# Expert weights in 1 MB loads of two rows to a partition, with every second factor column

## The chip, the cores and the metric

The kernel runs on one core of one Trainium2 chip. TensorE (PE) multiplies; VectorE (DVE), ScalarE (ACT) and GpSimd (POOL) do the elementwise work; SyncE (SP) issues most of the DMA transfers, and 16 DMA engines move the bytes between HBM and the on-chip SBUF. The metric is the device time of one execution in microseconds.

## What is computed

A two-layer transformer block in fp32 on 512 latent tokens (x) and 256 context tokens (ctx), 1024 wide. Each layer has a mixer (layer 0: dense attention and a convolution; layer 1: windowed attention and pooling) and then a mixture of experts with two of 32 experts for each token:

```python
def _moe(h, grp_w, grp_b, exp_w, exp_b, w_gate, w_up, w_down):
    ...  # a group of 8 experts by argmax, in it the two best, with weights
    def run(args):
        tok, wt, e = args
        xb = h_pad[tok]
        hid = jax.nn.silu(xb @ w_gate[e]) * (xb @ w_up[e])
        return (hid @ w_down[e]) * wt[:, None]
    ...

def reference(...):
    for i in range(DEPTH):              # 2
        ...                             # modulation from c, mixer, residual
        hx = _modulate(_rmsnorm(x, ln2_g[i]), sh2, sc2)
        ...
        x = x + g2 * out                # layer 0: 768 tokens; layer 1: 512
```

An expert has two factors of 1024 x 512 (w_gate, w_up) and one of 512 x 1024 (w_down), 6.3 MB; 32 experts are 201 MB a layer, and all of them are read.

## The kernel before

The order of the work is written out by hand on every engine, except that in two regions (layer 1's attention is one) PE, DVE and POOL are placed by a scheduler. The parts follow each other: mixer of layer 0, experts of layer 0, mixer of layer 1, experts of layer 1.

**Pages.** Large operands lie in SBUF pages of 128 x 1024 fp32 (4 KB to a partition, 512 KB). Class Pages keeps a list of free ones: 22 of pool keep for the whole program (R), and others that a part adds (T for 9 or 11 and S for 9 or 6 during the experts, by NT and NS; M and E in the mixer of layer 1). Pages.new takes the first that fits; Pages.done gives one back, and the next user of that place waits for the old one's readers. Weights, activations X, the fp32r parts hi and lo (class Split), attention outputs oT and a row g2b all live in such pages.

**Expert weights.** The host lays an expert out as 12 pages: chunks 0 and 1 (gate and up, 4 pages each, one page for 128 rows of the factor, with 256 gate and 256 up columns twice) and chunk 2 (down, 4 pages). Experts.queue lists all 384 pages of a layer in the order of use. Experts.ahead takes pages from that list as long as places are free and has SP issue one DMA for each (L1342):

```python
n, i, p = self.queue.pop(0)
t = pages.new("w", pools=self.pools)
queue.dma_start(t, a["ex"][self.l, order[n], i, p])
```

It is called while the mixer still runs (extra_slot, before_experts: FIRST and G1 say how many pages), and then each time pages were used: in layer 0 (main0) after all 8 pages of gate and up, and after the 4 of down; in layer 1 (main1, used_page) after each page.

**An expert.** Rows of its tokens come by an indirect DMA that POOL issues (gather, L1367) into Xg. In transposed, 8 PE transposes (L1476) turn them into xt, 128 features to a block; in layer 1 the modulation is applied while they are copied out of PSUM (modulate_T, L689 and L691, factors from A2s and modT). mm_gate_up (L1492) multiplies: for each of 8 blocks k of features and both halves c of the array, the stationary operand is 64 tokens of xt, the moving one 512 columns of page k. hidden applies silu and the product; hidden_T (L1506) transposes the result in blocks of 128; mm_down (L1514) does the same with the 4 pages of down. An fp32 matmul is two PE instructions; the two halves c run side by side. In layer 0 an expert has a second block of tokens if more than 64 came to it, and results go by scatters (POOL, L1394) that add to xD in HBM. In layer 1 two experts' results are added to X by one-hot products (combine, L1440).

**Layer 1's start.** The end of its mixer (OutProj) interleaves with the routing of each token tile. SP's queue there holds expert pages, g1b (a row that DVE waits for, L636), more pages, g2b, and then all others. On POOL, rs (L266) of each tile and the running sums of the routing precede the first gather.

Of the kernel before, what the change touches and what calls it, by code (L numbers as in the profile page):

```python
# [7 lines left out]
F32 = mybir.dt.float32  # L8
# [36 lines left out]
G1 = 3  # L45
FIRST = ((11, 0, 2), (7, 3, 2))

NT = (9, 11)
NS = (9, 6)
# [21 lines left out]
def hybrid_dit_kernel(ctx: ExitStack, tc: tile.TileContext, a, out):  # L71
# [27 lines left out]
    class Pages:  # L99
# [3 lines left out]
        def __init__(self):  # L103
            self.free, self.held, self.first = [], {}, None

        def add(self, pool, name, n):
            self.free += [(pool, f"{name}{i}") for i in range(n)]

        def drop(self, pool):
            self.done([t for t, p in list(self.held.values()) if p[0] is pool])  # L110
            self.free = [p for p in self.free if p[0] is not pool]

        def new(self, name, dt=F32, shape=(128, PAGE), pools=None):
            fit = [i for i, p in enumerate(self.free) if pools is None or p[0] in pools]
            i = next((i for i in fit if self.free[i][0] is self.first), fit[0])
            pool, tag = place = self.free.pop(i)
            t = pool.tile(list(shape), dt, tag=tag, name=name, bufs=1)
            self.held[id(t)] = (t, place)
            return t

        def done(self, tiles):
            for t in tiles:
                self.free.append(self.held.pop(id(t))[1])
# [112 lines left out]
    def mod_rows(l, name, src):  # L236
# [5 lines left out]
        for r in range(2):  # L242
            nc.sync.dma_start(rowD[l][name][r].rearrange("(k n) -> k n", n=128), g[r:r + 15:2, :])
# [35 lines left out]
    class Split:  # L279
# [15 lines left out]
        def low(self, t, eng=nc.vector):  # L295
            lo = pages.new("wl", F32R)
# [384 lines left out]

    def modulate_T(l, r, h, ps, dst):

        for i in range(4):
            k = h * 4 + i
            src = ps[:, i * 128:(i + 1) * 128]
            g, b = A2s[l][:, k, r:r + 1], modT[:, l, 24 + k, r:r + 1]
            if i % 2:
                nc.vector.tensor_scalar(dst[:, k, :], src, g, b, op0=OP.mult, op1=OP.add)  # L689
            else:  # L690
                nc.scalar.activation(dst[:, k, :], src, AF.Identity, bias=b, scale=g)  # L691
# [444 lines left out]
    class Router:  # L1136
# [107 lines left out]
        def slots(self, pool, work, room):  # L1244
# [3 lines left out]
            if self.l == 1:  # L1248
                self.iota = pool.tile([128, nt * 128], F32, name="iotaf")
                it = work.tile([128, nt * 128], I32, tag="ys", name="iotai", bufs=1)  # L1250
# [21 lines left out]
            def products():  # L1272
# [13 lines left out]
                pages.done([room])  # L1286
# [34 lines left out]

    class Experts:
        def __init__(self, l, nt, pools):
# [6 lines left out]
            self.queue = [(n, i, p) for n, i in self.queue + [(NE - 1, 2)] for p in range(4)]  # L1330
# [138 lines left out]
        def transposed(self, src, b, xt=None):  # L1469
# [3 lines left out]
            for h in range(2):  # L1473
                ps = sm("xtp")
                for k in range(4):
                    nc.tensor.transpose(ps[:, k * 128:(k + 1) * 128], src[:, (h * 4 + k) * 128:(h * 4 + k + 1) * 128], ident)  # L1476
                if self.l == 1:
                    modulate_T(1, 0, h, ps, xt)
# [8 lines left out]

        def mm_gate_up(self, b, xt, q, w, beside=lambda k: None):
# [22 lines left out]
        def mm_down(self, yy, b, t, w, beside=lambda f: None):  # L1511
            for f in range(4):
                for c in range(2):
                    nc.tensor.matmul(yy[c * 64:(c + 1) * 64], t[:, b, f % 2, f // 2, :],  # L1514
                                     w[f][:, c * 512:(c + 1) * 512], start=(f == 0), stop=(f == 3))
                beside(f)

        def begin(self):
# [6 lines left out]
            room = pages.new("slots", BF, (128, 2 * PAGE))  # L1525
# [30 lines left out]
        def main0(self):  # L1556
# [38 lines left out]
            pages.done(self.g2b)  # L1595
# [617 lines left out]
```

## Time and profile before

| | us |
|---|---|
| median of three runs | 1738.57 (1738.44 to 1743.09) |
| the profiled execution | 1740.23 |
| its span, first to last instruction | 1738.6 |
| PE busy | 1555.6 (89%) |
| DVE, ACT, POOL busy | 871.4, 498.0, 430.3 |
| mean granted TensorE clock | 0.965 of full speed |
| bytes moved by DMA | 518.65 MB, 488.58 MB of it on SP's queue |

Most durations here are from the one profiled execution. Its layer stages, read from when the expert products run: mixer of layer 0 until about 450 us, experts until about 955 us, mixer of layer 1 until about 1250 us, experts until the end. PE counts as busy while a matmul waits in its pipeline for data that a later one needs, so a full PE is not PE at its full pace; instructions in a stretch say more of its pace.

### The profile page before, as it was taken

The numbers are of one execution on the slowest core, as the hardware profiler recorded it, in microseconds if no ns is written. First come the engines' busy times: TensorE is split into PE (matmuls) and PEld (weight loads), VectorE is DVE, ScalarE is ACT, GpSimd is POOL, SyncE is SP. The second block draws the span as 40 slices with busy tenths as digits, with TensorE's granted clock in tenths as the row PEclk, the third lists the DMA queues.
The fourth block names the chain that finished last, engine by engine and source line by source line (L and its number), as shares of the span: only waits on it lengthen the run. The fifth ranks groups of instructions, "written<-read, shape, count | busy, mean of one in ns | idle before, by whom it ended". The sixth has DMA issues, their size and how long they took to land. (4 is left out here: it accounts for less than half of the span.)

```text
span 1738.6 us, 23632 instructions
## 1 busy us (share of the span) xinstructions
PE 1555.6 (89%) x8524; PEld 823.2 (47%) x8524; DVE 871.4 (50%) x1674; ACT 498.0 (29%) x998; POOL 430.3 (25%) x376
## 2 busy tenths in 40 slices
PE   5979689998799999999987589989699999999996
PEld 4868457887333333333322477668433343232332
DVE  3797889788333332233232565775533443343334
ACT  3422458833111111111111443482211211111111
POOL 2535555132122122112111222310112212121110
PEclk9999889999799999999999899999799999999998
DMA  9211833356899999999999524623899999999996
GB/s 369 64 65 69 314 135 147 110 197 238 333 392 398 400 385 383 397 388 389 397 394 397 218 74 181 239 89 131 319 410 409 408 409 408 408 408 408 408 410 235
DMA packets 151567, 518.65 MB, mean 298 GB/s; under 512 B 22444, under 2 KB 23180, under 8 KB 151436
## 3 DMA queue, kind: packets, MB, share of 16 engines
q1 hardware_dynamic: 136748, 488.58, 71.8%
q0 software_dynamic: 11520, 16.81, 3.7%
q10 hardware_dynamic: 3168, 11.54, 1.7%
q8 instruction: 79, 1.29, 0.3%
q14 instruction: 52, 0.43, 0.1%
HBM read 510.49 MB, written 21.02 MB: 306 GB/s over the span
## 5 line engine op out<-in xcount | busy, mean ns | idle before, releaser
L1492 PE MATMUL gu<-w,xt 128*64 128x512 f32 x2304 | 535.4, 602 | 23.4 <-DMA w<-in_ex_dram 19.1
L1492 PEld LDWEIGHTS gu<-w,xt 128*64 128x64 f32 x2304 | 151.2, 137 | 348.1 <-issue 240.8
L1514 PE MATMUL yy<-w,ht 128*64 128x512 f32 x1152 | 272.5, 608 | 15.4 <-DMA w<-in_ex_dram 6.6
L1499 DVE TENSOR_TENSOR hh<-hh,gu 128x512 f32<-128x512 f32 (+1 forms) x64 | 35.4, 553 | 356.2 <-ACT hh L1498 356.2
L1498 ACT ACTIVATE hh<-gu 128x512 f32<-128x512 f32 (+1 forms) x64 | 31.4, 490 | 612.5 <-PE gu L1492 336.9
L1514 PEld LDWEIGHTS yy<-w,ht 128*64 128x64 f32 x1152 | 78.1, 138 | 183.5 <-issue 133.3
L1394 POOL DMA_INDIRECT xD<-ys,sidx x40 | 71.1, 1777 | 317.0 <-DVE ys L1390 314.5
L1405 DVE TENSOR_TENSOR X<-X,cmb 128x512 f32<-128x512 f32 x126 | 79.6, 683 | 99.9 <-PE cmb L1440 99.8
L1424 POOL TENSOR_TENSOR lo<-ys,hi 64x512 fp32r<-64x512 f32 x58 | 72.5, 1268 | 217.0 <-ACT hi L1423 217.0
L1367 POOL DMA_INDIRECT Xg<-hD,gidx x40 | 41.9, 1048 | 263.2 <-PE xtp L1476 243.6
L751 DVE SCALAR_TENSOR_TENSOR acc<-glu,convp,acc 128x784 f32<-128x784 f32 x76 | 97.9, 1288 | 1.6
L762 POOL TENSOR_TENSOR part<-part,prod 128x784 f32<-128x784 f32 x40 | 84.7, 2118 | 43.2 <-ACT prod L761 42.3
L1390 DVE TENSOR_TENSOR ys<-yy,ys 128x512 f32<-128x512 f32 x64 | 44.3, 692 | 96.9 <-PEq L1305 52.8
L266 POOL TENSOR_TENSOR rs<-ms,mhalf 128x1 f32<-128x1 f32 (+2 forms) x40 | 41.4, 1036 | 170.8 <-DVE ms L264 170.2
L1423 ACT ACTIVATE hi<-ys 64x512 fp32r<-64x512 f32 x64 | 40.2, 629 | 139.7 <-DVE ys L1401 139.7
L524 PE MATMUL ptp<-cst,P 128*128 128x128 f32 x368 | 52.9, 283 | 18.6 <-POOL P L512 10.5
L1508 DVE COPY ht<-htp 128x512 f32<-128x512 f32 (+1 forms) x64 | 35.4, 553 | 66.6 <-PE htp L1506 66.6
L697 PE MATMUL qps<-wh,hi 128*128 128x256 f32 (+1 forms) x176 | 61.0, 347 | 8.0 <-DVE hi L1863 2.4
L532 ACT ACTIVATE pT<-ptp 128x512 f32<-128x512 f32 (+1 forms) x96 | 53.3, 589 | 44.8 <-PE ptp L524 44.1
L512 POOL TENSOR_SCALAR P<-P,rd 128x768 f32<-128x768 f32 (+3 forms) x40 | 33.2, 829 | 130.9 <-DVE rd L510 41.9
L502 ACT ACTIVATE P<-S,nm 128x768 f32<-128x768 f32 (+3 forms) x80 | 59.9, 757 | 13.1 <-DVE nm L495 8.3
L495 DVE TENSOR_REDUCE nm<-S 128x1 f32<-128x768 f32 (+3 forms) x80 | 58.6, 763 | 8.2 <-PE S L488 5.9
(310 smaller groups left out, 2551.2 us busy)
## 6 DMA issues: line engine op xcount, KB each, us to landing
w<-in_ex_dram SPq DMA_DIRECT2D x768, 512.0 KB
w<-in_mod_w_dram SPq DMA_DIRECT2D x96, 512.0 KB
w<-in_w_out_dram SPq DMA_DIRECT2D x16, 512.0 KB
w<-in_w_in_ab_dram SPq DMA_DIRECT2D x14, 512.0 KB
hD<-x ACTq DMA_DIRECT2D x8, 512.0 KB
xD<-X ACTq DMA_DIRECT2D x6, 512.0 KB
w<-in_w_in_cd_dram ACTq DMA_DIRECT2D x6, 512.0 KB
X<-xD SPq DMA_DIRECT2D x6, 512.0 KB
```

The source lines that it names most:

```text
L495: nc.vector.tensor_reduce(nm, u["S"][h][:, u["span"]], AX.X, OP.max, negate=True)
L502: nc.scalar.activation(u["P"][h][:, :n], u["S"][h][:, u["span"]], AF.Exp, bias=nm, accum_out=u["den"][:, h:h + 1])
L524: nc.tensor.transpose(ps[:, (c - c0) * 128:(c - c0 + 1) * 128], u["P"][c // nk][:, c % nk * 128:(c % nk + 1) * 128], ident)
L532: nc.scalar.activation(dst, src, AF.Copy)
L697: nc.tensor.matmul(ps[:, o:o + n], h(x, k, tk), w(p, k, 0, n), start=(k == 0 and c == 0), stop=(k == KT - 1 and c == 2))
L751: nc.vector.scalar_tensor_tensor(acc, glu[:, ct, i:i + CW], w(i), acc, OP.mult, OP.add)
L762: nc.gpsimd.tensor_tensor(self.part[ct], self.part[ct], t, OP.add)
L1394: return nc.gpsimd.indirect_dma_start(out=xD[:, :], out_offset=bass.IndirectOffsetOnAxis(ap=idx, axis=0), in_=ys[:, :], in_offset=None, bo ...
L1405: nc.vector.tensor_tensor(x, x, ps, OP.add)
L1424: eng.tensor_tensor(lo[rows, c], ys[rows, c], hi[rows, c].bitcast(F32), OP.subtract)
L1492: nc.tensor.matmul(self.gu[c * 64:(c + 1) * 64, b, :], xt[:, k, q * 64:(q + 1) * 64], w[k][:, c * 512:(c + 1) * 512], start=(k == 0), stop ...
L1514: nc.tensor.matmul(yy[c * 64:(c + 1) * 64], t[:, b, f % 2, f // 2, :], w[f][:, c * 512:(c + 1) * 512], start=(f == 0), stop=(f == 3))
```

## The change

Two pages of a chunk are now loaded by one DMA of 1 MB. A partition p takes rows 2p and 2p + 1 of a stretch of 256 rows of the factor, which lie behind each other in HBM: a run of 8 KB to a partition where two of 4 KB were. A matmul contracts 128 rows at a time, so the moving operand of block k is now the even or the odd rows of such a stretch (second_rows), and the features of block k must be every second column: the transposes read every second column of Xg and hh (every_second). In layer 1 the modulation factors then belong to other partitions; the rows A2 and B2 are written to HBM in the mixer and read back in that order into gb on POOL's queue.

SBUF places are now 8 KB to a partition with two halves. Experts.ahead takes whole places (Pages.pair); a page elsewhere takes a half, with rules on which half shares a tile with which. Counts change: G1, FIRST, NT, NS. Pages are given back by pairs in layer 1. g2b and slots no longer lie in pages. The last chunk of modulation weights in layer 1's mixer comes as three pages and a fourth after the loop.

```diff
-G1 = 3
-FIRST = ((11, 0, 2), (7, 3, 2))
-
-NT = (9, 11)
-NS = (9, 6)
+G1 = 2
+FIRST = ((5, 0), (3, 2))
+
+NT = (8, 10)
+NS = (8, 6)
...
     def add(self, pool, name, n):
-        self.free += [(pool, f"{name}{i}") for i in range(n)]
+        self.free += [(pool, f"{name}{i}", h) for i in range(n // 2) for h in range(2)]
+        if n % 2:
+            self.free.append((pool, f"{name}odd", 0))
...
+        def take(self, name, place, halves, dt):
+            if not self.used(place):
+                n = PAGE * (1 if place[1].endswith("odd") else 2)
+                self.base[place] = place[0].tile([128, n], dt, tag=place[1], name=name, bufs=1), dt, name
+            h = halves[0] * PAGE
+            t = self.base[place][0][:, h:h + PAGE * len(halves)]
...
+        def pair(self, pools):
+            t, places = self.take("w", self.whole(pools)[0], (0, 1), F32)
+            self.held[id(t)] = (t, places)
+            return t
...
+    def every_second(src, k):
+        return src.rearrange("p (j q s) -> p j s q", s=2, q=128)[:, k // 2, k % 2, :]
+
+    def second_rows(w, k, c):
+        o = k % 2 * PAGE + c * 512
+        return w[k // 2][:, o:o + 512]
...
-            while self.queue and most != 0 and len(pages.free) > spare and any(p[0] in self.pools for p in pages.free):
+            while self.queue and most != 0 and len(pages.free) > spare + 1 and pages.whole(self.pools):
                 n, i, p = self.queue.pop(0)
-                t = pages.new("w", pools=self.pools)
+                t = pages.pair(self.pools)
                 self.W.setdefault((n, i), []).append(t)
-                queue.dma_start(t, a["ex"][self.l, order[n], i, p])
+                queue.dma_start(t, a["ex"][self.l, order[n], i, 2 * p:2 * p + 2].rearrange("i (h s) n -> (i h) (s n)", s=2))
...
-                    nc.tensor.transpose(ps[:, k * 128:(k + 1) * 128], src[:, (h * 4 + k) * 128:(h * 4 + k + 1) * 128], ident)
+                    nc.tensor.transpose(ps[:, k * 128:(k + 1) * 128], every_second(src[:, :], h * 4 + k), ident)
...
+                src, g, b = ps[:, i * 128:(i + 1) * 128], self.gb[:, 0, k:k + 1], self.gb[:, 1, k:k + 1]
...
-                                     w[k][:, c * 512:(c + 1) * 512], start=(k == 0), stop=(k == KT - 1))
+                                     second_rows(w, k, c), start=(k == 0), stop=(k == KT - 1))
...
-                    nc.tensor.transpose(ps[:, (2 * b + c) * 128:(2 * b + c + 1) * 128], hh[:, b, c * 128:(c + 1) * 128], ident)
+                    nc.tensor.transpose(ps[:, (2 * b + c) * 128:(2 * b + c + 1) * 128], every_second(hh[:, b, :], c), ident)
...
             def beside(n, k):
-                self.used_page((n, k // 4), k % 4)
+                if k % 2:
+                    self.used_page((n, k // 4), k % 4 // 2)
...
-            t = pages.new("g2b", pools=[keep])
+            t = self.pools[1].tile([128, D], F32, name="g2b")
             self.g2b = [t]
             if self.l == 1:
                 row_bcast(1, "g2", 0, t)
+                self.gb = self.pools[1].tile([128, 2, KT], F32, name="gb")
+                for i, name in enumerate(("A2", "B2")):
+                    nc.gpsimd.dma_start(self.gb[:, i, :].rearrange("p (j s) -> p j s", s=2),
+                                        rowD[1][name][0].rearrange("(j p s) -> p j s", p=128, s=2))
```

On SP, at the passage from layer 0's mixer to its experts (X and g to B2b are the mixer's, g2b the experts'; a row's shape is partitions x columns, and a number at its end counts repeats), before:

```order
L144 DMA X<-in_x_dram 128x1024 x3
L1342 DMA w<-in_ex_dram 128x1024 x5
L144 DMA X<-in_x_dram 128x1024
...
L1342 DMA w<-in_ex_dram 128x1024 x11
L1667 DMA g2b<-rowg_87 64x512 x4
L1342 DMA w<-in_ex_dram 128x1024 x12
L1305 UNCONDITIONAL_BRANCH
L1342 DMA w<-in_ex_dram 128x1024 x6
L1305 UNCONDITIONAL_BRANCH
L1342 DMA w<-in_ex_dram 128x1024 x4
```

and after:

```order
L188 DMA X<-in_x_dram 128x1024 x3
L1385 DMA w<-in_ex_dram 128x2048 x2
L188 DMA X<-in_x_dram 128x1024
...
L1385 DMA w<-in_ex_dram 128x2048 x6
L1724 DMA g2b<-rowg_87 64x512 x4
L1385 DMA w<-in_ex_dram 128x2048 x6
L1337 UNCONDITIONAL_BRANCH
L1385 DMA w<-in_ex_dram 128x2048 x3
L1337 UNCONDITIONAL_BRANCH
L1385 DMA w<-in_ex_dram 128x2048 x2
```

The 38 pages at this passage are 19 pairs, and four pages where five were stand ahead of the mixer's last X.

On SP, at the passage from layer 1's mixer to its experts, before:

```order
L243 DMA rowg_91<-grow 8x128 x2
L1342 DMA w<-in_ex_dram 128x1024 x14
L258 DMA g1b<-rowg_88 128x1024
L1342 DMA w<-in_ex_dram 128x1024 x3
L258 DMA g2b<-rowg_91 128x1024
L1342 DMA w<-in_ex_dram 128x1024 x367
```

and after:

```order
L287 DMA rowg_91<-grow 8x128 x2
L1385 DMA w<-in_ex_dram 128x2048 x6
L302 DMA g1b<-rowg_88 128x1024
L1385 DMA w<-in_ex_dram 128x2048 x2
L302 DMA g2b<-rowg_91 128x1024
L1385 DMA w<-in_ex_dram 128x2048 x184
```

Ahead of g1b stand 12 pages instead of 14, ahead of g2b 16 instead of 17.

On POOL, in the same passage (rhs, sums: the routing's running sums; rs: a tile's norm; gb: the new factors), after:

```order
L310 TENSOR_TENSOR rs<-ms,mhalf 128x1
L1205 TENSOR_SCALAR rhs<-O,cst 128x2x32
L1206 TENSOR_SCALAR rhs<-O 128x2x32
L1718 DMA gb<-rowA_89 128x4x2
L1718 DMA gb<-rowB_90 128x4x2
L1223 TENSOR_TENSOR sums<-sums,O 128x32
L1224 TENSOR_TENSOR sums<-sums,O 128x32
L310 TENSOR_TENSOR rs<-ms,mhalf 128x1
```

The two loads of gb stand between the sums of the third token tile and the norm of the last; before, nothing stood there.

## Rows read from the trace of the kernel before

**Rows 1.** Page: busy time by engine; DMA share in 40 slices, tenths.

```profile
PE 1555.6 (89%) x8524; PEld 823.2 (47%) x8524; DVE 871.4 (50%) x1674; ACT 498.0 (29%) x998; POOL 430.3 (25%) x376
...
DMA  9211833356899999999999524623899999999996
```

**Rows 2.** Stretches: length; PE, PEld, DVE, ACT, POOL busy (instructions); clock, DMA, GB/s.

```profile
450.00:480.00 30.00, 28.16 (x135) 11.21 (x135) 6.84 (x14) 4.35 (x8) 2.57 (x3) 0.93 0.77 295
520.00:800.00 280.00, 273.94 (x1340) 101.62 (x1338) 84.24 (x126) 43.77 (x72) 55.52 (x38) 1.00 1.03 392
800.00:955.00 155.00, 132.79 (x594) 41.52 (x592) 45.01 (x68) 22.68 (x37) 24.20 (x15) 0.99 1.03 394
1240.00:1260.00 20.00, 11.48 (x46) 4.61 (x46) 8.28 (x35) 3.90 (x9) 4.54 (x5) 0.67 0.74 257
1260.00:1420.00 160.00, 158.81 (x728) 60.90 (x730) 63.44 (x122) 28.75 (x58) 33.59 (x28) 1.00 1.03 409
1420.00:1715.00 295.00, 278.35 (x1176) 93.36 (x1174) 111.22 (x202) 47.52 (x94) 52.05 (x43) 0.99 1.02 407
```

**Rows 3.** SP's waits: total, times, longest; 500 to 955, 1260 to 1715 us.

```profile
SPq L1342 <- DMA w<-in_ex_dram: 317.4, 304, 2.2
...
SPq L1342 <- DMA w<-in_ex_dram: 298.3, 325, 1.9
```

**Rows 4.** SP's waits, 1240 to 1260 us.

```profile
SPq L1342 <- PE gu L1492: 14.3, 5, 10.9
```

**Rows 5.** DMA by queue (q1: SP): packets, MB, share; 480-955, 1260-1712 us.

```profile
q1 hardware_dynamic: 48010, 174.82, 92.4%
...
q1 hardware_dynamic: 49671, 180.86, 100.4%
```

**Rows 6.** DMA packets, 1450-1460 us; ACT's queue q10, 1230-1240 us.

```profile
DMA packets 1130, 4.11 MB, mean 411 GB/s; under 512 B 126, under 2 KB 126, under 8 KB 1130
...
q1 hardware_dynamic: 1130, 4.11, 103.2%
...
q10 hardware_dynamic: 144, 0.52, 12.9%
```

**Rows 7.** DMA packets, 1731 to 1737 us, the output's stores.

```profile
DMA packets 1051, 1.89 MB, mean 315 GB/s; under 512 B 128, under 2 KB 128, under 8 KB 1051
...
q1 hardware_dynamic: 1051, 1.89, 84.8%
```

**Rows 8.** Page, part 3; then 0.4 us from 1505.5 and from 604.5 us.

```profile
q14 instruction: 52, 0.43, 0.1%
...
q14 instruction: 1, 0.01, 4.9%
...
q14 instruction: 1, 0.01, 4.8%
```

**Rows 9.** PE in order of time, 600 to 625 us: start, duration, instructions.

```profile
607.44 7.09 PE L1492 MATMUL gu<-w,xt 128*64 128x512 f32 x32
```

**Rows 10.** PE in order of time, 1214-1262 us (idle time in brackets).

```profile
1247.97 1.97 PE L1476 MATMUL xtp<-cst,Xg 128*128 128x128 f32 x8 [8.78 <-DMA Xg<-hD,gidx]
```

**Rows 11.** DVE, then PE in order of time, 1165 to 1200 us.

```profile
1185.81 0.69 DVE L636 TENSOR_TENSOR otmp<-ops,g1b 128x512 f32<-128x512 f32 x1 [11.67 <-DMA g1b<-rowg]
...
1188.32 1.03 PE L647 MATMUL h2p<-cst,X 128*128 128x128 f32 x8
```

**Rows 12.** POOL in order of time, 1195-1262 us; POOL's groups, the gather.

```profile
1231.55 0.55 POOL L266 TENSOR_TENSOR rs<-ms,mhalf 128x1 f32<-128x1 f32 x1 [4.35 <-DVE ms L264]
...
L1367 POOL DMA_INDIRECT Xg<-hD,gidx x40 | 41.9, 1048 | 263.2 <-PE xtp L1476 243.6 <-PE yy L1514 11.7 <-DVE wgs L1239 2.7
```

**Rows 13.** Tiles xtp, htp: duration min/median/max, ns; PE in order, 560-580.

```profile
L1476 PEld LDWEIGHTS xtp<-cst,Xg x384: 138/141/230, 448.6 to 1681.9; 128*128 128x128 f32 x192
...
L1506 PEld LDWEIGHTS htp<-cst,hh x192: 137/140/145, 468.8 to 1719.2; 128*128 128x128 f32 x192
...
566.08 1.94 PE L1476 MATMUL xtp<-cst,Xg 128*128 128x128 f32 x16 [0.31 <-PEq L1305]
```

More of the change, by code (lines that the diff above doesn't have):

```diff
@@ L111, in drop, with whole @@
             self.free = [p for p in self.free if p[0] is not pool]
[L113 to L118, printed above, removed]
+        def whole(self, pools):
+            seen, fit = set(), []
+            for p in self.free:
+                if p[:2] in seen:
+                    fit.append(p[:2])
+                seen.add(p[:2])
+            return [p for p in fit if pools is None or p[0] in pools]
@@ new lines, in used @@
+        def used(self, place):
+            return any(p[:2] == place for _, ps in self.held.values() for p in ps)
+        def take(self, name, place, halves, dt):
[4 more added lines that the diff above has]
+            t = self.base[place][0][:, h:h + PAGE * len(halves)]
+            for k in halves:
+                self.free.remove((*place, k))
+            return t, [(*place, k) for k in halves]
@@ new lines, in pair, with new @@
+        def pair(self, pools):
+            t, places = self.take("w", self.whole(pools)[0], (0, 1), F32)
+            self.held[id(t)] = (t, places)
+            return t
+        def new(self, name, dt=F32, shape=(128, PAGE), pools=None, mate=None):
+            d = F32R if dt is F32R else F32
+            fit = [p for p in self.free if pools is None or p[0] in pools]
+            old = [p for p in fit if self.used(p[:2]) and self.base[p[:2]][1] is d]
+            new = [p for p in fit if not self.used(p[:2])]
+            if name == "oT":
+                new.sort(key=lambda p: p[1].endswith("odd"))
+            same = [p for p in old if self.base[p[:2]][2] == name]
+            fit = [p for p in same + new if p[0] is self.first] + same + new + old
+            place = fit[0]
+            if mate is not None:
+                q = self.held[id(mate)][1][0]
+                other = (*q[:2], 1 - q[2])
+                place = other if other in self.free else place
+            t, places = self.take(name, place[:2], (place[2],), d)
+            if len(shape) > 2:
+                dims = "abcd"[:len(shape) - 1]
+                t = t.rearrange(f"p ({' '.join(dims)}) -> p {' '.join(dims)}", **dict(zip(dims[1:], shape[2:])))
+            self.held[id(t)] = (t, places)
@@ L241, in mod_rows @@
         nc.vector.tensor_copy(g, ps[0:16, 0:128])
-        for r in range(2):
-            nc.sync.dma_start(rowD[l][name][r].rearrange("(k n) -> k n", n=128), g[r:r + 15:2, :])
+        for r in range(n):
+            queue.dma_start(rowD[l][name][r].rearrange("(k n) -> k n", n=128), g[r:r + 15:2, :])
     biasD = [dram.tile([2, 36], F32, name=f"bias{l}") for l in range(2)]
@@ L1329, in __init__ @@
                 self.queue += chunks[2:] + chunks[:2] if n == NE - 1 else chunks
-            self.queue = [(n, i, p) for n, i in self.queue + [(NE - 1, 2)] for p in range(4)]
+            self.queue = [(n, i, p) for n, i in self.queue + [(NE - 1, 2)] for p in range(2)]
         def router(self, work):
@@ L1524, in begin @@
             self.gather0(1)
-            room = pages.new("slots", BF, (128, 2 * PAGE))
+            room = (self.wp if l else self.pool).tile([128, 2 * PAGE], BF, tag="ys" if l else "slots", name="slots", bufs=1)
             self.ahead()
@@ L1695, in rest @@
             own = float(FIRSTB[l] * BLK)
-            W = [pages.new("w") for _ in range(12)]
+            W = [pages.pair(None) for _ in range(6)]
             xr = pages.new("xt", shape=(128, KT, 128))
@@ L1937, in mixer_cd_in @@
             w.done()
+        mods[-1] += load(a["mod_w"][1, todo[0] - 1, 3:], 1, [keep, m1])
         warm(AF.Exp)
```

53 lines of the change are left out of this document (27 added, 26 removed).

## The prediction

> **What bounds the kernel now.** I read the page's busy shares and slices first. PE is busy for 89% of the span, but the row of DMA slices has two long runs of 9 [rows 1]: about 450 to 955 us (experts of layer 0) and 1215 to 1715 us (experts of layer 1). So next the table of stretches [rows 2]. In both stages the DMA engines are full (share 1.03) at 392 to 394 GB/s and at 407 to 409 GB/s, in the first half of a stage and in the second. PE goes through the first half without a gap: 1340 matmuls in 280 us (4.79 per us) in layer 0, 728 in 160 us (4.55 per us) in layer 1. In the second half it falls to 594 in 155 us (3.83) and 1176 in 295 us (3.99). It has eaten the pages loaded ahead and now goes at the pace of the DMA. Most of that stall is hidden inside matmuls that the profile counts as busy. From the other side: SP, which issues every page, waits for the DMA queue and hardly for PE [rows 3]: 304 and 325 times, as each issue waits for an earlier transfer to land (the SP order with its waits shows eight semaphores in turn). Only just after each stage begins, 450 to 480 and 1240 to 1260 us, do pages run out, and SP waits for PE to free some (14.3 us in layer 1) [rows 4]; DMA is then 0.77 and 0.74 busy [rows 2].
>
> So the end of each stage is the time at which the last weight lands, and that is bytes through a full DMA. PE without stalls would do the 594 matmuls in 594/4.79 = 124 us, so it would end 31 us earlier in layer 0; in layer 1 1176/4.55 = 258 us, 37 us earlier. That is how much a faster DMA can bring before PE takes over.
>
> **Part 1: 8 KB runs.** What does a packet cost? In the packet counts by queue, the share times 16 engines times the stretch is the packets' time. From 1450 to 1460 us SP's queue spent 1.032 x 160 = 165.1 us on 1130 packets; 126 are under 512 B, and at nothing for these a 4 KB packet took 164 ns [rows 6]. ACT's queue in ten other us (0.129 x 160 us; its 0.52 MB are 128 packets of 4 KB, the rest small) gives 161 ns [rows 6]. The stores of the end have 2 KB packets: 0.848 x 96 = 81.4 us for 923, 88 ns each [rows 7]. Two of 2 KB cost 12 ns more than one of 4 KB, so a packet has a fixed price. 8 KB packets are in the trace too: queue q14 fetches instructions, 52 packets with 0.43 MB, and a single one within a full stretch of 0.4 us takes 4.9 or 4.8% of 6.4 us: 312 ns as a mean of four such stretches, three of them at 4.9% [rows 8]. Two 4 KB packets are 322 to 328 ns, so a merged pair saves 10 to 16 ns; the step from 2 to 4 KB says 12. I take 11, near the low rows, since q14 moves to another place; the bounds are 6 and 17.
>
> An engine moves a megabyte at 409 GB/s in 2.564 us. With eight packets for sixteen it saves 8 x 11 ns, over 1.03 for the overlap, 85 ns: 3.3% (422 GB/s); the bounds give 1.8 and 5.1%. It holds for SP's queue alone: 92.4 of 103% in layer 0 from 480 to 955 us, 100.4 of 103% in layer 1 from 1260 to 1712 us [rows 5]. Layer 0: 475 x 0.897 x 3.3% = 14.1 us; layer 1: 452 x 0.975 x 3.3% = 14.5 us. **Together -28.6 us** (-16 to -44), both below the 31 and 37 us at which PE takes over. All of it lies on the path that sets the end.
>
> [...]
>
> **Part 2: twice as much in one issue.** SP has half the issues, and each waited for the DMA queue anyway. What comes late: PE gets two pages at once. At a stage's end it then has two k steps left after the last landing instead of one. 32 matmuls take 7.09 us [rows 9], a page is four matmuls, 0.86 us: **+1.7 us** for two layers. Gathers and activation stores that share an engine now sit behind 8 KB packets, not 4 KB ones: about 150 ns more for each of the 4 to 8 packets an engine has. It shows only where PE waits for the first gather of a layer, 8.8 us in layer 1 [rows 10]: **+2 us** for both (0 to 3).
>
> **Part 3: places and counts.** SBUF pages go from 22+9+9 and 22+11+6 to 22+8+8 and 22+10+6, but g2b and slots leave them. The SP order shows what stays ahead: in layer 0 5+11+12+6+4 = 38 pages before the first issue that waits for expert 0's products, and 2+6+6+3+2 = 19 pairs now, the same; in layer 1 33 pages and 17 pairs. So the gaps of [rows 4] stay, at nothing. In the mixers a place is reused when both halves are free; PE, ACT and DVE keep their order there but for some instructions of layer 1's attention. A place may come free later than a page did, or sooner, since one wait serves two loads. The nearest row is g1b, which SP issues after the experts' pages: DVE waited 11.7 us for it, until 1185.8 us, while PE had products until past 1188 us [rows 11]. A few us later, and PE waits as well. **+3 us** for mixers (-5 to +8).
>
> **Part 4: factors in every second column.** In layer 1 two small stores and two loads (gb, 512 runs of 8 bytes each) go on POOL. POOL has 4.35 us free at that place, before rs of the last tile, and a gather (128 indices) takes it 1.05 us [rows 12]. Two loads fit if they take under 2.1 us each, so I put them at nothing; at four times a gather's price, for 512 runs, they are 8.4 us, a delay of 4 us. The transposes now load their stationary operand from every second column: 384 xtp and 192 htp, 141 and 140 ns a load, in the shade of matmuls, 16 of which take 1.94 us, 121 ns each [rows 13]. The trace has no strided load. The bounds are nothing and a doubled load with no cover, 576 x 141 ns = 81 us of PE; I take nothing, as a load need only keep to its row. Moving operands stay contiguous, in 512 columns.
>
> **The sum.** The profiled execution took 1740.2 us for a span of 1738.6; -28.6 + 1.7 + 2 + 3 = -21.9 gives 1718.3. The median of the three runs, 1738.6, lies 1.7 us lower: **1716.6, forecast 1717 us**, 1704 to 1729 by the bounds of parts 1, 3 and 4.
>
> **Rivals.**
> *Runs are cut.* If the queue splits a row into 4 KB packets, nothing is saved and the 6.7 us of costs stay: 1745 us. For: no SP or ACT packet in the trace is over 4 KB. Against: none asked for more, and the instruction queues do carry 8 KB in one. This is the case that the change doesn't do what it says. 0.11.
> *Strided loads make PE the bound* (the one that ends slower by a mechanism). At the full price layer 0 gets 256 + 128 transposes x 141 ns = 54 us: PE ends at 924 + 54 = 978 us and not 955, +23. Layer 1 gets 27 us: 1678 + 27 = 1705, against 1715 now, -10. With 6.7 of costs, +20: 1758 us. The total turns slower from about 98 ns a transpose, 70% of a whole load. 0.07, as it needs nearly the whole bound. [...]
> *The fixed price is a third as large.* The 2 KB rows are stores and the 8 KB rows instruction fetches; if weight loads save only 4 ns a pair, 1.2% or 10 us go: 1735 us. 0.06, since three kinds of rows say 10 or more. [...]
> *Mixers give it back.* If pages that must wait for both halves make PE wait in both mixers, g1b first, by 15 us more than I put: 1732 us. 0.06.
>
> **How the numbers follow.** Forecast 0.70, rivals 0.11, 0.07, 0.06, 0.06. The range 1704 to 1741 leaves out 0.03 below, and above most of the cut runs and the strided loads, 0.17. About 0.3%, 5.2 us, can be told from no change. Faster (under 1733.4): 0.69 of the forecast, 0.035 of the mixers, 0.015 of the third: 0.74. Slower (over 1743.8): 0.07 of the cut runs, 0.06 of the strided loads: 0.13. Within: 0.13.
>
> **What would show it.** In the profile after, SP's queue should have some 55,000 fewer packets and most bytes in packets of 8 KB; GB/s near 420 in layer 1 and 405 in layer 0; the stages about 14 us shorter each; SP still waiting for DMA, not PE. If packets stay at 4 KB, the first rival holds; if DMA share falls under 1 in a stage while transposes take over 200 ns each, the second. Wrong would be a rate that rises while the end stays.

## The result, and the profile after

The changed kernel takes 1730.44 us (median of 4 runs, 1727.03 to 1736.64) against 1739.99 beside it: ratio 0.994, 95% interval 0.9923 to 0.9957. Measured once more with six runs it was 1730.26 us, 0.9921 (0.9906 to 0.9937). The forecast was 1717. The direction was right and the time lies inside the range, but the gain is 10 to 14 us where 21.6 was forecast.

The profiled execution is the slowest of the first four (1736.64 us, span 1735.0). The page, to be read beside [rows 1], busy time by engine and DMA share in 40 slices:

```profile
PE 1557.7 (90%) x8526; PEld 851.2 (49%) x8526; DVE 869.0 (50%) x1676; ACT 498.3 (29%) x998; POOL 430.1 (25%) x380
...
DMA  9211744256799999999999514704899999999995
...
q1 hardware_dynamic: 81452, 488.56, 69.5%
```

SP's queue has 55,296 packets fewer (136,748 before). The two runs of 9 are still there, and the first begins a slice later. The same stretches as in [rows 2], with PE, PEld, DVE, ACT, POOL, then granted clock, DMA share and GB/s:

```profile
450.00:480.00 30.00, 24.05 (x106) 9.98 (x106) 5.47 (x16) 1.79 (x3) 0.99 (x1) 0.81 0.68 273
520.00:800.00 280.00, 273.97 (x1317) 104.11 (x1314) 81.02 (x120) 41.40 (x68) 53.06 (x36) 1.00 1.02 406
1260.00:1420.00 160.00, 158.26 (x722) 62.63 (x720) 64.07 (x130) 27.86 (x57) 31.09 (x26) 1.00 1.00 409
1420.00:1715.00 295.00, 279.10 (x1224) 106.96 (x1220) 115.27 (x209) 49.26 (x98) 54.58 (x45) 0.99 1.00 413
```

In the middle of layer 0 the rate is 406 GB/s where it was 392 [rows 2]. In the middle of layer 1 it is 420 where it was 408, from 1320 to 1600 us, before and after:

```profile
1320.00:1600.00 280.00, 271.17 (x1189) 97.38 (x1187) 110.45 (x203) 48.37 (x97) 57.64 (x48) 1.00 1.03 408
```

```profile
1320.00:1600.00 280.00, 274.22 (x1222) 107.91 (x1218) 113.21 (x207) 49.67 (x99) 60.17 (x50) 0.99 1.01 420
```

So the bytes run as forecast. But 450 to 480 us has 106 matmuls where there were 135, and 273 GB/s where there were 295. PE's first rows say why (start, duration, idle time before it in brackets). Before, in layer 0 (layer 1 is in [rows 10]):

```profile
448.62 3.94 PE L1476 MATMUL xtp<-cst,Xg 128*128 128x128 f32 x16
452.49 14.83 PE L1492 MATMUL gu<-w,xt 128*64 128x512 f32 x64
```

After, in both layers:

```profile
453.28 1.98 PE L1519 MATMUL xtp<-cst,Xg 128*128 128x128 f32 x8 [3.20 <-DMA Xg<-hD,gidx]
456.55 1.95 PE L1519 MATMUL xtp<-cst,Xg 128*128 128x128 f32 x8 [1.28 <-DMA Xg<-hD,gidx]
458.43 15.39 PE L1545 MATMUL gu<-w,xt 128*64 128x512 f32 x64
...
1254.59 1.98 PE L1519 MATMUL xtp<-cst,Xg 128*128 128x128 f32 x8 [11.55 <-DMA Xg<-hD,gidx]
1256.51 8.84 PE L1545 MATMUL gu<-w,xt 128*64 128x512 f32 x32
```

The first expert product starts at 458.4 us in layer 0, where it was 452.5, and at 1256.5 in layer 1 (1249.9). Both wait for gathered rows. SP meanwhile has filled its places and waits for PE. Its waits for gate and up products (total, times, longest) from 450 to 490 us, before and after, with a DMA share of 0.83 and 0.65 in that stretch:

```profile
SPq L1342 <- PE gu L1492: 13.3, 8, 10.2
```

```profile
SPq L1385 <- PE gu L1545: 29.1, 4, 25.1
```

To see where time goes I cut the execution at four events: the issue of the last store of normed rows (hD, on ACT), the first expert product, the end of expert 30 in layer 0 (up to there its weights set the pace), the last gate or up product in layer 1. In us, each stretch by itself; "again" is a second profiled execution of the changed kernel (span 1723.5):

| stretch | before | after | again | split | start2k | hold |
|---|---|---|---|---|---|---|
| start to store, layer 0 | 433.4 | 434.8 | 433.5 | 430.4 | 431.9 | 434.2 |
| store to first product | 19.0 | 23.6 | 24.0 | 20.4 | 17.8 | 18.7 |
| to the end of expert 30 | 498.8 | 492.4 | 491.6 | 504.2 | 488.9 | 489.0 |
| to the end of layer 0 | 16.6 | 21.2 | 16.7 | 16.7 | 17.1 | 18.2 |
| mixer of layer 1, to its store | 265.5 | 265.2 | 262.7 | 262.8 | 262.0 | 262.0 |
| store to first product | 16.6 | 19.3 | 19.0 | 16.6 | 17.3 | 16.3 |
| to the last gate and up product | 465.7 | 455.4 | 454.6 | 466.5 | 455.2 | 454.4 |
| to the end | 23.0 | 23.1 | 21.4 | 21.4 | 22.7 | 21.4 |

The stages are 7 and 11 us shorter, not 14 each, and the two starts give back 4.8 and 2.6 (means of after and again). The 21.2 us at the end of layer 0 belong to that one execution: the last expert ran partly at the lower clock. Its 32 products before, after, and in "again":

```profile
954.12 7.09 PE L1492 MATMUL gu<-w,xt 128*64 128x512 f32 x32 [2.87 <-DVEq L1700]
```

```profile
953.66 10.07 PE L1545 MATMUL gu<-w,xt 128*64 128x512 f32 x32 [2.87 <-DVEq L1757]
```

```profile
952.01 7.09 PE L1545 MATMUL gu<-w,xt 128*64 128x512 f32 x32 [2.88 <-DVEq L1757]
```

The granted clock from 950 to 960 us was 0.66 of full speed in the second (0.50 from 953 to 957 us), and 1.00 in the others.

### The profile page after: what moved, and what is told of

It reads as the page before. It is cut to its first block, busy times and chain, and to the rows that moved or that the text cites. A ratio compares the mean times of both kernels' runs of the same rounds, so it can differ in the third digit from the quotient of the medians.

```text
span 1735.0 us, 22803 instructions
## 1 busy us (share of the span) xinstructions
PE 1557.7 (90%) x8526; PEld 851.2 (49%) x8526; DVE 869.0 (50%) x1676; ACT 498.3 (29%) x998; POOL 430.1 (25%) x380
## 5 line engine op out<-in xcount | busy, mean ns | idle before, releaser
L1545 PE MATMUL gu<-w,xt 128*64 128x512 f32 x2304 | 526.8, 604 | 15.8 <-DMA w<-in_ex_dram 12.9
L1545 PEld LDWEIGHTS gu<-w,xt 128*64 128x64 f32 x2304 | 157.8, 138 | 322.2 <-issue 274.1
L1567 PE MATMUL yy<-w,ht 128*64 128x512 f32 x1152 | 267.1, 606 | 15.2 <-DMA w<-in_ex_dram 7.6
L730 PE MATMUL qps<-wh,hi 128*128 128x256 f32 (+1 forms) x352 | 90.0, 348 | 9.2 <-DVE hi L1921 2.4
L672 PE MATMUL ops<-wh,fh 128*128 128x512 f32 x288 | 85.3, 402 | 0.0
L1519 PE MATMUL xtp<-cst,Xg 128*128 128x128 f32 x384 | 55.1, 295 | 20.7 <-DMA Xg<-hD,gidx 16.0
L730 PEld LDWEIGHTS qps<-wh,hi 128*128 128x128 f32 x352 | 63.0, 200 | 18.1 <-DVE hi L1921 2.6
L1519 PEld LDWEIGHTS xtp<-cst,Xg 128*128 128x128 f32 x384 | 51.4, 209 | 36.2 <-PEq L1337 17.4
L568 PE MATMUL ptp<-cst,P 128*128 128x128 f32 x368 | 52.8, 282 | 16.5 <-POOL P L556 7.7
```

Of the source, the lines that this page charges most:

```text
L568: nc.tensor.transpose(ps[:, (c - c0) * 128:(c - c0 + 1) * 128], u["P"][c // nk][:, c % nk * 128:(c % nk + 1) * 128], ident)
L672: nc.tensor.matmul(s["ps"][:, h * 512:(h + 1) * 512], f[x][:, k, :], self.wo[h](p, k, 0, 512), start=(k == 0 and c == 0), stop=(k == KT - ...
L730: nc.tensor.matmul(ps[:, o:o + n], h(x, k, tk), w(p, k, 0, n), start=(k == 0 and c == 0), stop=(k == KT - 1 and c == 2))
L1519: nc.tensor.transpose(ps[:, k * 128:(k + 1) * 128], every_second(src[:, :], h * 4 + k), ident)
```

## The experiments

**First theory: late starts.** The store hD and the first gathers share the DMA engines with weights. If an engine serves one packet of each queue in turn, a store's packet now waits for an 8 KB packet instead of a 4 KB one. Rivals: the dearer strided weight loads, or loads that come by pairs.

*again* is the changed kernel itself.

> The changed kernel once more, unaltered, for a closer ratio and a second profile. Theory (late start): the DMA rate rose as forecast, but the store of the normed rows (hD) and the first gathers of each layer now wait behind 8 KB packets, so PE's first expert product starts later than before (452.5 us in layer 0, 1249.9 in layer 1) by 4 to 6 us in each layer, and SP, whose places are all full by then, lets the DMA engines run dry for 5 to 8 us more in layer 0. Expected: 1728 to 1733 us, ratio 0.992 to 0.996, first product of layer 0 at 456 to 459 us, DMA share from 450 to 490 us at 0.6 to 0.7. Rival (dearer weight loads on the path, 209 ns for 141): the start of the stage is where it was and the loss is spread over the stage: matmuls per us in the DMA-bound half lower than the rate of bytes allows. Rival (1 MB at a time): PE's waits for weights at the end of a stage grow from 0.2 to over 1 us each.

1730.26 us; first product at 457.6 us, DMA share 0.66 from 450 to 490 us. Loads by pairs did not make PE wait longer for weights: before the gate and up products the page of the changed kernel has 12.9 us of it, the page before 19.1.

*split* loads a pair by two DMAs:

```diff
-queue.dma_start(t, rows.rearrange("i (h s) n -> (i h) (s n)", s=2))
+for s in range(2):
+    queue.dma_start(t[:, s * PAGE:(s + 1) * PAGE], rows.rearrange("i (h s) n -> (i h) s n", s=2)[:, s, :])
```

> The changed kernel, but each pair is loaded by two DMAs, one for the first and one for the second row of every partition: the same places, pairs, releases, strided transposes and factors, with 4 KB packets. Theory (late start): rate back to 392 and 409 GB/s, and with it the packets ahead of the store and the gathers shrink again: PE's first product of layer 0 at 453 to 455 us (1.3 us of a later mixer stay), of layer 1 no more than 4 us behind that of before; time 1738 to 1745 us, within 0.3% of before. Rival (dearer weight loads on the path): slower than before by their price, 1750 us or more. Rival (pairs and places cost): slower than before by 5 to 12 us with the start of layer 0 still at 456 us or later.

1744.75 us, ratio 1.0007 (0.9995 to 1.002). Rate 391 and 409 GB/s, store to first product 20.4 and 16.6 us. So the gain goes with the split, and places, pairs and counts bring none in the sum. Most of the late start goes with it too: all of it in layer 1, and in layer 0 3.4 of 4.8 us; why 1.4 us stay is open. In this one execution layer 0's stage is 5 us longer than before (504.2) and the two mixers 6 us shorter; which of pairs, places and counts makes the stage longer was not tried. Split changes two things at once: the packets are half as long, and SP's eight loads in flight hold 4 MB, not 8. What speaks for the packet are the packets' counts and times further down.

*plainT* takes both stationary operands from consecutive columns:

```diff
-nc.tensor.transpose(..., every_second(src[:, :], h * 4 + k), ident)
+nc.tensor.transpose(..., src[:, (h * 4 + k) * 128:(h * 4 + k + 1) * 128], ident)
```

> The changed kernel with the stationary operands of the expert transposes taken from consecutive columns, as in the kernel before, while the factors keep the rows of the change, so the products are of other rows than asked for; all else is the same. Theory (late start): a weight load falls from 209 to 141 ns, but it lies beside matmuls: time within 2 us of the changed kernel, 1727 to 1733 us. Rival (dearer weight loads on the path): 576 x 68 ns = 39 us come off PE, and if a quarter of that were on the path the time falls by 10 us, to 1720.

1730.19 us: the same as the changed kernel. The tile's rows in the changed kernel and in plainT (duration min/median/max in ns):

```profile
L1519 PEld LDWEIGHTS xtp<-cst,Xg x384: 194/209/231, 453.3 to 1679.6; 128*128 128x128 f32 x192
```

```profile
L1519 PEld LDWEIGHTS xtp<-cst,Xg x384: 138/141/231, 451.0 to 1674.0; 128*128 128x128 f32 x192
```

A strided load costs 68 ns more, half of a load and not nothing, but it lies beside matmuls.

*split_start* uses split's two DMAs for the 11th to 19th pair of layer 0 and the 10th to 17th of layer 1 alone.

> The changed kernel, but only the pairs that are in flight while each stage starts (the 11th to 19th of layer 0, the 10th to 17th of layer 1) are loaded by two DMAs with 4 KB packets. Theory (late start): the store and the gathers are as quick as before, PE's first product comes 3 to 5 us earlier in layer 0 and 2 to 3 us in layer 1 than in the changed kernel, the rate of the rest stays at 406 and 420 GB/s; time 4 to 8 us below the changed kernel, 1722 to 1727. Rival (1 MB at a time, or weight loads): no gain from it, 1729 to 1733, even where the start comes earlier.

1723.13 us, ratio 0.9886 (0.9867 to 0.9906); store to first product 21.1 and 17.2 us, the rest still at 406 and 420 GB/s.

*start2k* loads those pairs by four DMAs with 2 KB packets.

> The changed kernel, but the pairs in flight while a stage starts (11th to 19th in layer 0, 10th to 17th in layer 1) come in four DMAs each with 2 KB packets; the rest in 8 KB packets. Theory (each packet of the store and of a gather waits for one packet of the weights): the eight packets of the store on each engine take 8 x (159 + 85) = 2.0 us and not 3.7; from the issue of the store to PE's first product in layer 0 under 20 us (8 KB: 23.8, 4 KB in split_start: 21.1), in layer 1 under 16.5 (19.1 and 17.2); time at or 1 to 3 us below that of split_start, 1720 to 1723. Rival (the delay came from the 8 MB in flight, not from the length of a packet): no better than split_start, or worse by the poorer rate of 2 KB packets.

1722.66 us, 0.9899 (0.9871 to 0.9928); 17.8 us in layer 0 and 17.3 in layer 1. In layer 0 the start follows the packet: 23.8 us at 8 KB, 21.1 at 4, 17.8 at 2. In layer 1, where I expected under 16.5, it does not get shorter below 4 KB. The reason for layer 0 stands in the packet counts by queue while the store runs (q10 is the store, q1 the weights: packets, MB, share). Before, 1237 to 1239 us; after, 439 to 441; start2k, 436 to 437.5:

```profile
q10 hardware_dynamic: 108, 0.44, 53.9%
q1 hardware_dynamic: 107, 0.40, 49.1%
```

```profile
q1 hardware_dynamic: 65, 0.53, 63.6%
q10 hardware_dynamic: 72, 0.29, 35.8%
```

```profile
q10 hardware_dynamic: 104, 0.43, 69.0%
q1 hardware_dynamic: 103, 0.20, 34.0%
```

In these rows it is one packet of each in turn, be the weights' packets of 4, 8 or 2 KB. From its first packet to its last the store took 2.65 us, 4.03 and 2.29; eight packets an engine, each with one of the other queue, are 8 x (161 + 164) = 2.6, 8 x (161 + 315) = 3.8 and 8 x (161 + 91) = 2.0 us (161 ns from [rows 6], the others from below). All 16 engines were done with their eight packets at the end of the store, 3.4 to 4.0 us after its first packet in the changed kernel, 2.4 to 2.8 before and 1.8 to 2.3 in start2k; an engine that served its eight in a row would need 8 x 161 ns = 1.3 us. So the packet accounts for the store's delay; the gathers were not timed in this way.

*hold* leaves the last four pairs that layer 0 loads ahead, and the last two of layer 1, to ACT:

```diff
-            self.ahead()
+            self.ahead((3, 2)[l])
...
             if l == 0:
                 self.trans(0, 1)
+            self.ahead(queue=nc.scalar)
```

> The changed kernel, but the last four pairs that layer 0 loads ahead, and the last two of layer 1, are issued by ACT behind the copy of the first transposed rows and not by SP ahead of them, so that fewer weights share the engines with the first gathers. Packets and sizes are those of the change. Theory (late start): first product 2 to 4 us earlier after the store in layer 0 than in the changed kernel, 1 to 2 us in layer 1; the idle time of the DMA lies ahead of the stage instead of behind its start: 2 to 6 us below the changed kernel. Rival (what counts is only when the pages are full): later loads push the stage back, 0 to 5 us above the changed kernel.

1720.29 us, 0.9881 (0.9856 to 0.9906): first product 5 and 2.7 us sooner than in the changed kernel. Not the rival: the later loads did not push the stages back.

*before_hold* does the same to the kernel before (eight and four pages).

> The kernel before, with 4 KB packets, but the last eight pages that layer 0 loads ahead and the last four of layer 1 are issued by ACT behind the copy of the first transposed rows, as in hold. Theory (late start): the delay by packets of weights is there before the change too, at half the size: store to first product 16.5 to 18 us in layer 0 (19.0) and 15.5 to 16.3 in layer 1 (16.6); 1 to 5 us faster than before, against the 10 us by which hold was faster than the changed kernel. Rival (hold gains by something of its own, whatever the packet): as much as in the changed kernel, 8 to 10 us.

1738.78 us against 1742.4, 0.9976 (0.9964 to 0.9987); 18.0 and 14.3 us. So the delay was there before the change; to avoid it was worth 3.6 us, about a third of what hold gains over the changed kernel.

**Second theory: the engines run apart.** Why did the stage of layer 0 lose only 7 us at 3.6% more bytes per second? When the last down factor that PE has to wait for had landed (expert 29's; the expectations below call it expert 30's), 253.3 MB had gone through SP's queue, 251.2 before. I took the 2 MB for work done too early on some engines while the last one was waited for, caused by 8 MB in flight.

*halves* keeps 8 KB packets but has 4 MB in flight (SP's eight loads are half as large):

```diff
+for h in range(2):
+    queue.dma_start(t[h * 64:(h + 1) * 64, :], rows[h * 64:(h + 1) * 64, :])
```

*both* adds split_start's loads at the stages' starts to it.

> The changed kernel, but each pair is loaded by two DMAs of 64 partitions each: the packets stay at 8 KB, what eight DMAs in flight hold falls from 8 MB to 4 MB, as in the kernel before. Theory (late start by 8 KB packets): the store and the gathers stay slow, from the issue of the store to PE's first product 23 to 24 us in layer 0 and 19 in layer 1. Theory on the end of layer 0 (engines apart): in the changed kernel 253.2 MB had gone through SP's queue when the last down factor but one landed, 251.2 MB in the kernel before; the DMA engines run further apart when 8 MB are in flight, and the last engine counts. With 4 MB in flight the expert stage of layer 0, from its first product to the end of expert 30, should take 486 to 489 us and not 492; time 3 to 5 us below the changed kernel. Rival (it is the end of a pair, or places): 492 us as in the changed kernel, same time. Rival (the depth delays the gathers): store to first product back to 20 and 17 us.

> The changed kernel with the pairs in flight at a stage's start loaded as in split_start (two DMAs of 4 KB packets) and all others as in halves (two DMAs of 64 partitions, 8 KB packets, 4 MB in flight). Theory (late start, and engines apart at the end of layer 0): both gains add up, 8 to 12 us below the changed kernel, 1718 to 1722. Rival (engines apart does not count): as split_start, 1723.

Some 2,300 us, both of them. From 520 to 800 us of halves:

```profile
520.00:800.00 280.00, 208.86 (x870) 72.76 (x872) 57.42 (x86) 28.76 (x48) 37.18 (x25) 0.91 1.02 258
```

The engines are full (share 1.02) at 258 GB/s, 0.64 of the 406 of the changed kernel, whose loads go to 128 partitions. So these two say nothing on the question.

*split_end* gets 4 MB in flight in another way: the last 24 pairs of layer 0 come as in split.

> The changed kernel, but the last 24 pairs of layer 0 (experts 28 to 31) come in two DMAs each with 4 KB packets, so that 4 MB and not 8 MB are in flight there, with all 128 partitions in each. Theory (engines apart at the end of layer 0): when the last down pair of expert 30 landed, 253.1 to 253.3 MB had gone through SP's queue in every run with 1 MB DMAs, 251.2 and 250.4 MB in the kernel before and in split. Here about 251 MB; the stage of layer 0, from its first product to the end of expert 30, shrinks from 492 us by 2 MB / 406 GB/s = 5 us less the 24 x 69 ns = 1.7 us of the shorter packets, to 488 to 490; time 1 to 4 us below the changed kernel. Rival (a pair lands later because it is a pair, or the count only reflects the order of issue): 492 to 494 us, time 0 to 3 us above the changed kernel.

1729.1 us, 0.9929 (0.9913 to 0.9945). The bytes fell to 250.9 MB, as expected, the stage did not get shorter: 492.1 us. The theory falls: the 2 MB are there, but cost nothing that this shows. They only make the GB/s look better than the load that lands last.

The trace marks when each of the 16 engines has finished its part of a load. From these marks, in us (pairs counted from 0 in each layer; spread is the median, last engine less first, of the loads issued from 700 to 800 us):

| | before | split | after | noscat4 | noscat8 |
|---|---|---|---|---|---|
| layer 0, pair 40 to 180, last engine | 402.5 | 404.1 | 394.4 | 374.6 | 367.4 |
| the same, first engine | 400.4 | 401.9 | 381.9 | 372.0 | 366.8 |
| layer 1, pair 40 to 191, last engine | 396.5 | 396.1 | 385.2 | 396.1 | 384.6 |
| spread, layer 0 | 7.0 | 6.9 | 16.9 | 6.4 | 2.7 |

The last engine gained 2.0% in layer 0, the first 4.6%; in layer 1 the last gained 2.8%. The 4.6% are no rate: the first engine ran ahead once, from 4 us ahead of the last at pair 44 to 15 at pair 100, and from there to pair 180 both take 222 us. The stretch from 520 to 800 us holds this running ahead, so its 3.6% more bytes per second are too good. *noscat8* and *noscat4* drop the scatters of layer 0, from the changed kernel and from split (one execution each):

```diff
 def store():
+    if n:
+        return
     st = self.add_rows(ys, sidx[:, b, e:e + 1])
```

> The changed kernel without the scatters of layer 0's experts (all but the first expert's are left out, so its sums are missing in xD). In the changed kernel the DMA engines run apart in layer 0: of one load the first engine is done 16 to 17 us before the last (4 to 8 us in layer 1), and from the 40th to the 180th pair of layer 0 the last engine became only 2.0% quicker by the change (402.5 to 394.4 us), the first 4.6%. Theory (the scatters lie on some engines more than on others, and what they cost there is not shortened by longer runs): spread in layer 0 down to 4 to 8 us, the 40th to the 180th pair in 358 to 366 us, as in layer 1 (2.55 us a pair), and against noscat4 2.6 to 3.0% quicker. Rival (the scatters are not it): spread stays at 15 us, 2.0% quicker than noscat4.

> The same with split, that is with 4 KB packets: no scatters in layer 0 but the first expert's. Theory (scatters): the 40th to the 180th pair in 367 to 375 us (2.63 us a pair as in layer 1), spread 4 to 7 us; noscat8 is 2.6 to 3.0% quicker. Rival (not the scatters): 395 to 404 us, and noscat8 2.0% quicker.

The scatters cost the last engine 404.1 - 374.6 = 29.5 us at 4 KB packets. The spread of the changed kernel goes from 16.9 to 2.7 us without them, but that doesn't show that they drive the engines apart: in noscat8 PE became the bound, and while SP waited for PE (151.5 and 61.9 us, below), an engine that was late may have caught up. In noscat4, where SP still waits for the DMA, the spread stays (6.4 us, 6.9 in split). For the scatters speaks layer 1 of the changed kernel, with 8 MB in flight and no scatters: a median of 6.6 us for the loads issued from 1450 to 1550 us (5.3 in again). So this is argued, not shown. The size of the gain without scatters (1.9%) says nothing either, for the same reason. SP's waits, 600 to 940 us, in the changed kernel and in noscat8:

```profile
SPq L1385 <- DMA w<-in_ex_dram: 287.0, 120, 3.4
```

```profile
SPq L1385 <- PEq L1337: 151.5, 30, 7.4
SPq L1385 <- PE gu L1547: 61.9, 20, 9.0
```

If the scatters' time is not shortened by the change, 2.8% of the other 374.6 is 10.5 us; split to after has 9.7. That fits, but it is worked out, not shown.

**The packet's price.** *all2k* loads every pair by four DMAs with 2 KB packets.

> The changed kernel with each pair loaded by four DMAs of 2 KB packets. Fixed price of a packet as I had it (11 to 12 ns, from 2 KB at 85 to 88, 4 KB at 161 to 164 and 8 KB at 312 ns): 381 to 390 GB/s in layer 1 (4 KB: 409, 8 KB: 420), and both stages 20 to 25 us longer than with 4 KB packets; time 1780 to 1795 us, PE's first product 17 to 18 us after the store in layer 0. Rival (8.6 ns a packet, which is what 420 against 408.5 GB/s says): 388 to 392 GB/s in layer 1, time 1770 to 1778.

1825.69 us, 371 GB/s from 1320 to 1600 us: dearer than both theories. Packets of SP's queue from 1450 to 1460 us, in the changed kernel and in all2k (packets under 512 B: 64 of q1's in the first, 229 in the second):

```profile
q1 hardware_dynamic: 574, 4.18, 100.5%
```

```profile
q1 hardware_dynamic: 2056, 3.74, 103.7%
```

An 8 KB packet takes 1.005 x 160 us / 510 = 315 ns, a 2 KB one 1.037 x 160 / 1827 = 91. By these means merging saves 2 x 91 - 164 = 18 ns from 2 to 4 KB and 13 from 4 to 8, and there it pays even less in bytes: 409 to 420 GB/s is 2.564 to 2.497 us an engine and megabyte, 8.4 ns a pair. The means hold stretched packets, and time in which packets of one engine overlap, of which the long ones have less: the DMA share of a full layer 1 is 1.03 before and 1.01 after. The commonest duration of a packet on SP's queue is plainer: 84, 159 and 309 ns for 2, 4 and 8 KB in all2k, the kernel before and the changed one, from 600 to 800 us (two thirds to three quarters of the packets) and again from 1320 to 1600, and 9 ns for a packet of 4 bytes. That is 9 ns for any packet and 150 for each 4 KB, so a merged pair saves 9 ns.

**Better versions.** *best* puts hold, start2k (11th to 15th pair) and split_end together.

> Everything together: the last pairs ahead issued by ACT behind the first transposed rows as in hold, the pairs ahead of them (11th to 15th of each layer) in 2 KB packets as in start2k, the last 24 pairs of layer 0 in 4 KB packets as in split_end, all others in 8 KB packets. Theory (late start): store to first product about 16 us in layer 0 and 15.5 in layer 1, the stages themselves as long as in hold or 2 to 3 us shorter in layer 0; 1712 to 1718 us. Rival (the gains are the same idle time of the DMA counted twice): as hold, 1720.

1726.38 us, 0.9903 (0.9885 to 0.9922): the gains don't add up. Store to first product was 20.0 us in layer 0, worse than in hold; why is open.

*hold_all* gives all seven and all four to ACT, *hold_again* is hold.

> As hold, but all seven pairs of layer 0 and all four of layer 1 that were asked for behind the first gathers are issued by ACT behind the first transposed rows, not four and two. Theory (late start): store to first product another 1 to 2 us earlier in layer 0 (18.7 in hold, 24 in the changed kernel), but the DMA engines idle for about as long as three pairs take before it: time between 2 us below and 4 us above hold. Rival (when the pages are full is what counts): 5 us or more above hold.

> hold once more, for a closer interval: 1717 to 1724 us, ratio to the kernel before 0.986 to 0.990. If the gain over the changed kernel (0.9921 in its second measurement) was an accident of the first measurement: 0.990 to 0.993.

hold_all: 1723.17 us, 0.9894 (0.9876 to 0.9911). Its starts are no later (18.7 and 14.5 us), but its stages 6 and 5 us longer than hold's (495.0 and 459.6): here the later loads pushed the stages back. hold_again: 1718.04 us, 0.9865 (0.9845 to 0.9884). So hold beats both kernels, the changed one by 7 to 13 us, going by the ratios. The start of layer 0 in hold_again, 450 to 490 us, where the changed kernel has a DMA share of 0.65:

```profile
450.00:490.00 40.00, 38.22 (x184) 14.96 (x184) 9.35 (x16) 4.22 (x7) 6.43 (x5) 0.98 0.91 359
```

## Why the forecast was twice too large

*Part 1, -28.6 us, a step that failed in its size and took the larger share of the miss.* The mechanism held: packets became 8 KB, and the gain went with them (split). But the whole stages became only 6.8 and 10.7 us shorter (means of after and again), together -17.5. Measured by the load that lands last, between the pairs in the table, it is 402.5 to 394.4 us in layer 0 and 396.5 to 385.2 in layer 1, together -19.4, where the prediction's 3.3% would give 11.9 + 12.8 = 24.7. Two things were off. A merged pair saves 8.4 ns of the engine's time by bytes and 9 by the commonest packet, not 11: I compared means that hold overlapping and stretched packets, and kept the overlap at 1.03, while it fell to 1.01. And in layer 0 the gain was smaller still, 2.0% against 2.8%; that the scatters' part of the engines' time does not shrink fits it, but was not shown. The cover was smaller, too, though it did not come to matter: I let PE take over 31 us earlier, but noscat8, with PE as the bound, needs 481.1 us for the stage, only 18 less than before. The stretch from 800 to 955 us in [rows 2] held the end of the stage, where PE waits for other things.

*Part 2, +2 us for the first gathers: the step whose mechanism failed.* It was 4.8 + 2.6 = 7.4 us. The price of a packet, 150 ns (309 for 159), was right; I forgot that two transfers follow each other there, the store and then the gathers, and that the 150 ns fall on each of eight packets in each (for the gathers an estimate). That is 16 x 150 ns = 2.4 us, about what layer 1 lost. In layer 0 the store took 1.4 us longer (2.6 to 4.0 us), and some 3 us more were lost behind it, where POOL issues three gathers one after another (444.0, 445.6 and 446.9 us) and not two; how these divide was not measured, and 1.4 us of the 4.8 stay in split. I also looked for a wait in layer 1 only, where [rows 10] shows 8.8 us; in layer 0 the gather was just hidden, and that cover had no room: PE's 3.20 and 1.28 us of waiting are new. "The gaps stay, at nothing" held for the places, but a later PE makes the same gap longer.

*+1.7 us for pairs at the end:* not seen there; the stretches at the ends did not grow, but for the lower clock of that one execution. (Four of 32 matmuls in 7.09 us are 0.89 us, not 0.86.) Between split and before, pairs, places and counts together cost 5 us in layer 0's stage, 3.7 of them before the 40th pair, and 0.8 in layer 1's.

*Part 3, +3 us for the mixers:* +1.4 and +0.1 us in layer 0's mixer, -0.3 and -2.8 in layer 1's (after and again), so not seen. The wait for g1b can go either way: in the profiled execution DVE's first product with it begins at 1188.07 us after a wait for PE, in again it waits 9.26 us for g1b.

*Part 4, at nothing:* right. The two loads of gb, which stand ahead of the third tile's running sums, took POOL 0.88 and 0.77 us and left 2.37 us free ahead of rs; strided loads cost 68 ns each, under cover (plainT); that they would cost none was an assumption with no row behind it.

The sum with what was measured: -17.5 for the stages, +7.4 for their starts and +1.1 or -2.7 for the mixers (after, again) is -9.0 or -12.8 us; the two measurements have -9.5 and -13.7. Of the rivals none holds alone: packets were not cut, PE did not become the bound, the mixers gave nothing back; those of 1732 and 1735 us came nearest in time, but for other reasons. No run shows the 4 ns a pair of the rival at 1735 us; a pair saves the 8.4 to 9 ns above.

## What to carry to other kernels

Longer runs raised the rate of a full DMA by little here (409 to 420 GB/s from 4 to 8 KB), and the short store that shared the engines paid for it, a whole packet of the weights for each of its own (2.65 to 4.03 us). So look at the few transfers on which a stage's start waits, and issue the bulk that isn't needed yet behind them, but not so late that it holds up the stage (hold_all); here that was worth about as much as the longer runs. And read a full DMA by the load that lands last, not by bytes per second.

## What I had not expected of the hardware

While a store ran, the engines took single packets of two queues in turn (108 and 107, 72 and 65, 104 and 103). Loads to 64 partitions ran at 258 GB/s where 128 ran at 406. The commonest packet cost 9 ns and 150 for each 4 KB (84, 159 and 309 ns). Of a load in layer 0 the first engine was done 17 us before the last with 8 MB in flight, and 7 us with 4 MB. A stationary operand from every second fp32 column loaded in 209 ns and not in 141 (after and plainT), where I had put the difference at nothing.
